# Where the state-space tables are made, when side pieces are emitted, and which queue loads rows and x

## The chip, the cores and the metric

The kernel runs on one core of a Trainium2 chip. The metric is the device time of one execution in microseconds. Its engines are called by the names of the profile: PE (TensorE, the matmuls), DVE (VectorE), ACT (ScalarE), POOL (GpSimd) and SP (SyncE, which here only issues DMAs). DMAs are issued from the queues of SP, ACT and POOL; an engine works its own instructions, DMA issues among them, strictly in order.

## The reference

One layer of a hybrid trunk on a sequence of 512 with 2048 channels, in float32: an adaLN modulation, one wide projection, an S5 state-space mixer and a gated DeltaNet side by side, a gated merge, an output projection, and a SwiGLU feed-forward part.

```python
h  = LN0(x) * (1 + scale_m) + shift_m            # scale, shift, gates = c @ w_ada
p  = h @ W_in      # -> u_ssm | q | k | v | z | beta | a | gate_ssm | gate_gdn
ys = S5(u_ssm): 64 groups x 16 channels, 64 complex states each; GLU; -> 2048
yg = gated DeltaNet: 8 heads, dk = dv = 128, causal conv of 4, chunks of 64; -> 2048
m  = sigmoid(gate_ssm) * ys + sigmoid(gate_gdn) * yg
x  = LN1(alpha * x + gate_m * (m @ W_out))
h  = LN0(x) * (1 + scale_f) + shift_f
x  = LN2(alpha * x + gate_f * SwiGLU(h))
```

The part of S5 that depends on the parameters alone is made once; these are "the state-space tables" below:

```python
dt = exp(log_dt);  mag = exp(lr * dt);  ang = li * dt
ab_re, ab_im = mag * cos(ang), mag * sin(ang)
f = ((ab - 1) * conj(lam)) / |lam|^2             # and powers of ab for the scan
```

## The kernel before

**Matmuls.** Every large product is a float32 product made from three rounded ones (`mm3`, L1130): both sides are split into a high and a low part, and hi*hi, hi*lo and lo*hi go into the same PSUM tile. Such a triple of matmuls, of 512 columns each, is the unit in which the main work advances. Weights come through the class `Weights` (L933-1005): tiles of 512 KB (two halves of 128x1024) are loaded on SP into one of three `raw` buffers, ACT casts them to `whi`, DVE subtracts to `wlo`, and `run_ahead` and a poll keep this two tiles ahead of the matmuls.

**Stages.** The start stage loads x and 64 tiles of `w_ada` (512 KB each, named `wad`), sums the adaLN columns on DVE (`acc`) and PE (`px_adr`), normalizes x, makes h (`hf`, split into `at`), and computes the first six tiles of u. Then come the rest of u and eight DeltaNet heads (the loop at L1468-1480, four gemms each: q, k, v, z). The merge gates, the up-projections, GLU and the merge follow, then the mix-out product (L1687-1716), which goes through four quarters of 512 columns and, in each, twice through pairs of token tiles, so that `w_mix` is loaded twice. At the first pair of a quarter it loads the gate row of that quarter (`row_of`, L1594-1597, into the single buffer `grow`) and tiles of x (L1701). Layer norm halves follow with the rows `ln1_g`, `ln1_b` (L1639-1644). The feed-forward part (L1763-1781) uses `row_of` again, once per quarter and block.

**Side lines and the order.** All instructions go through wrappers (L170 for the engines' operations, L211 for matmuls, L216 for transposes), so most lines of the profile read L170 or L211. The wrappers record each instruction in the class `Order` (L57-152), which keeps a planned clock per engine, with planned durations (L174-189, for POOL 0.2 us plus 0.0021 or 0.0030 us per element of the row). Work beside the main matmuls is written as generators, "lines": the S5 tables `s5_setup` (L272-388), `s5_line` (L551, eight batches), three lines of the DeltaNet, the adaLN rows. After each triple of main matmuls `tick` looks at the lines and emits up to two steps of each line whose planned time `line.t` is far enough in the past:

```python
while n and not line.done and line.t + self.MARGIN <= self.clock:
```

`until` and `drain` emit without that. So the order on every engine is fixed when the kernel is built; on the chip the engines keep it and wait for one another by semaphores. The tables are a line added in the start stage (L1362) and drained at its end (L1395). Most of their arithmetic is on POOL, the sine and cosine on ACT (`sn`, `cs` from `sr`), four transposes on PE into `px_s`, and their results go into `PAr`, `Pi`, `Ftab` and others.

**The adaLN rows in the heads.** `ada_line` (L1167) with `pace` sums 16 tiles (`w1`, 256 KB) into `aacc` on DVE, one each 6.0 us by the plan, and keeps `depth` loads ahead from SP. Without pace it loads from POOL.

Of the kernel before, what the change touches and what calls it, by code (L numbers as in the profile page):

```python
# [11 lines left out]
F32 = mybir.dt.float32  # L12
# [36 lines left out]
def bc(ap, shape):  # L49
    return ap.to_broadcast(shape)  # L50
# [6 lines left out]
class Order:  # L57
# [5 lines left out]
    LAT = 0.12  # L63
    MARGIN = 0.4

# [943 lines left out]
def kernel(ctx, tc, x, c, w_ada, b_ada, w_in, lam_re, lam_im, log_dt, b_re, b_im, c_re, c_im,  # L1009
# [4 lines left out]
    pool_of = lambda **kw: tc.tile_pool(reuse_waits="tile", **kw)  # L1014
# [156 lines left out]
    def ada_line(p, col0, pace):  # L1171
# [7 lines left out]
        deep = k.ada_deep and not pace  # L1179
        depth = 3 if pace else 6 if deep else 4  # L1180
        eng = k.sync if pace else pool
# [60 lines left out]
    cmix = k.per5.tile([128, C_WIDTH - 128], F32, name="cmix")  # L1242
    start, set5 = ExitStack(), ExitStack()
    sp = start.enter_context(pool_of(name="start", bufs=1, side="right"))
    s5p = set5.enter_context(pool_of(name="s5set", bufs=1))
    xs = [[None] * 4 for _ in range(4)]
# [114 lines left out]
    ws.run_ahead()  # L1361
    s5s = o.add(s5_setup(k, s5p, lam_re, lam_im, log_dt))  # L1362
    xnT = []
# [20 lines left out]
    for g in range(4):  # L1384
        o.until(lambda: len(hT) >= 4 * g + 4)
        for k0, nk, cols, u0 in ((0, 2, 512, 0), (2, 2, 512, 0), (0, 4, 256, 4)):
# [7 lines left out]
            ws.run_ahead()  # L1394
    o.drain(s5s)  # L1395
    start.close()
    set5.close()

# [30 lines left out]
    k.tc = lambda n: gp.tile([128, 256], F32, name="g_" + n, tag=n, bufs=1 if n == "X" else 2)  # L1429
    k.sm5 = sp5 = sps.enter_context(pool_of(name="sp5", bufs=1))  # L1430
    alias5 = {"g": "X", "y": "S"}
    alias5w = {"G": "W", "H": "V", "R": "W"}
    k.t5 = lambda n: sp5.tile([128, 512], F32, name="s_" + n, tag="s" + alias5.get(n, n), bufs=2 if n == "U" else 1)
    k.t5w = lambda n: sp5.tile([128, 1024], F32, name="s_" + n, tag="s" + alias5w.get(n, n))
    k.u_done = 0
# [13 lines left out]
    for j in range(6):  # L1449
        u_out(upsum[j])  # L1450
    s5l = o.add(s5_line(k, (b_re, b_im, c_re, c_im), dcol))
    psb = [None]
# [29 lines left out]
    def switch():  # L1482

        o.drain(s5l)
        o.drain(gl)
        sps.close()
        gps.close()
        per5s.close()
        bp = ctx.enter_context(pool_of(name="bp", bufs=32))
        q2 = ctx.enter_context(pool_of(name="q2", bufs=2))  # L1490
        P2.extend((bp, q2))

        def operands():
            for dst, src in ((zs, k.dz), (ygs, k.dy)):
                r = load2(src[0])
                for j in range(8):
                    yield r
                    nxt = load2(src[j + 1]) if j < 7 else None
                    hi, lo = bt(), bt()
                    if dst is zs:  # L1500
                        act.copy(nat(hi), by_pos(r))
                        v.tensor_tensor(out=nat(lo), in0=by_pos(r), in1=nat(hi).bitcast(F32), op=S)
                    else:
                        split(hi, lo, r)
                    dst.append((hi, lo))
                    r = nxt
        k.ada_deep = True
        o.add(operands())
        o.add(ada_rest())
# [88 lines left out]
    def row_to(t, src, q):  # L1598
        ld.dma_start(out=t, in_=bc(src[0:1, 512 * q:512 * q + 512], [128, 512]))
        return t  # L1600
# [30 lines left out]
    def ln_half(hf):  # L1631
# [7 lines left out]
        def row(q):  # L1639
            rows.append((t2("gg"), t2("gs")))  # L1640
            for r, src in zip(rows[q], (ln1_g, ln1_b)):
                ld.dma_start(out=r, in_=bc(src[0:1, 512 * q:512 * q + 512], [128, 512]))
        row(0)
# [43 lines left out]
    for hf in range(2):  # L1687
        for q in range(4):
            sl = slice(512 * q, 512 * q + 512)
            pss = [psum_mm(), psum_mm()]  # L1690
            for c0 in range(0, 16, 2):
                hi, lo = ws.next(2, 512)
                for ti in range(2):
                    ts_ = slice(256 * hf + 128 * ti, 256 * hf + 128 * ti + 128)
                    if c0 == 4:
# [4 lines left out]
                        xa[t][q] = at(F32)  # L1700
                        ld.dma_start(out=xa[t][q], in_=x[0, 128 * t:128 * t + 128, sl])  # L1701
                    for i in range(2):
# [153 lines left out]
```

## Time and profile before

| | us |
|---|---|
| median of 3 runs (lowest to highest) | 3168.74 (3167.68 to 3170.12) |
| the profiled execution | 3170.34 |
| its span in the profile | 3168.6 |
| PE busy in it | 3033.4 (96%) |
| DVE, ACT, POOL busy | 1663.2, 954.5, 782.8 |
| mean granted clock of PE | 0.977 |

A row of the windows has the stretch and its length, then for each engine the busy time and in brackets the number of instructions, then the granted clock (PEclk, 1.00 is full), the mean busy share of the 16 DMA engines and the GB/s that they moved. PEld are PE's weight loads. A row of groups has line, engine, operation, output and inputs with shapes and count, then total and mean (ns) duration, then the idle time of the engine just before these instructions and what ended it. A row of waits reads "who waited <- for whom: total us, how often, longest". In the timeline the first two numbers are the start and the duration. Of a DMA issue the profile has the time of the issuing instruction on the queue's engine (ns: least, median, most) and the time to landing.

### The profile page before, as it was taken

Reading aid. Unit: us, or ns where it says so; the run is one execution under the profiler, and the core shown is the slowest. Engines: PE = TensorE matmul, PEld = TensorE weight load, DVE = VectorE, ACT = ScalarE, POOL = GpSimd, SP = SyncE. Lnnn points to the kernel's source line nnn. Section 1 sums busy time; section 2 is a strip of 40 time slices with the busy share of each in tenths; the row PEclk is TensorE's granted clock in tenths of the full one; section 3 lists DMA queues with packets and bytes.
Section 4 is the critical chain, followed back from the end, with each engine's and each line's share of the span. In section 5 each row is a group of like instructions: output and inputs, shape, how many; then the busy total and the mean of one; then the engine's idle time right before and its main releaser. Section 6 shows DMA issues by size and latency. Waiting matters only on the chain.

```text
span 3168.6 us, 40305 instructions
## 1 busy us (share of the span) xinstructions
PE 3033.4 (96%) x15953; PEld 2499.7 (79%) x15953; DVE 1663.2 (52%) x2217; ACT 954.5 (30%) x1378; POOL 782.8 (25%) x832
## 2 busy tenths in 40 slices
PE   5899989989999999999989999999999999999997
PEld 2588878778777878888769998888888888888885
DVE  6647777666554576756687543333333333333337
ACT  3233333333222343323345631222222222222121
POOL 4834655455112255100022102002001100200202
PEclk8899989999999999999999999999999999999998
DMA  9654334333332688656866553333333333333333
GB/s 330 229 148 110 98 87 111 105 105 95 117 109 84 201 288 288 224 188 207 261 225 192 169 170 103 100 97 110 94 99 110 97 100 101 105 95 102 109 101 120
DMA packets 513534, 458.14 MB, mean 145 GB/s; under 512 B 56145, under 2 KB 403633, under 8 KB 513345
## 3 DMA queue, kind: packets, MB, share of 16 engines
q1 hardware_dynamic: 495904, 408.91, 42.4%
q0 software_dynamic: 10240, 33.56, 3.1%
q10 hardware_dynamic: 7200, 13.10, 1.2%
q8 instruction: 125, 2.05, 0.3%
q14 instruction: 65, 0.52, 0.1%
HBM read 435.60 MB, written 19.89 MB: 144 GB/s over the span
## 4 chain that ended last, share of the span: by engine, by line
PE 64%; DMA 4%; DVE 4%; issue 2%; ACT 2%; POOL 1%; SPq 0%; ACTq 0%; DVEq 0%; POOLq 0%
PE pm L211 47%; PE px_fo L211 14%; DMA raw<-in_w_mix_out_dram 2%; PE px_gd L211 2%; DVE wlo L170 1%; ACT whi L170 1%; DVE at L170 1%; DMA w<-in_w_ada_dram 1%; DVE aacc L170 1%; PE px_ada L211 0%; DMA raw<-in_ffn_w_in_dram 0%; PE px_s L211 0%; ACT f L170 0%; DVE bt L170 0%; DMA g_G<-dG 0%
## 5 line engine op out<-in xcount | busy, mean ns | idle before, releaser
L211 PE MATMUL pm<-at,whi 128*128 128x512 f32 (+1 forms) x3744 | 1145.5, 389 | 8.0 <-ACT whi L170 5.0
L170 DVE TENSOR_TENSOR wlo<-raw,whi 128x1024 fp32r<-128x1024 f32 x541 | 683.4, 1265 | 800.6 <-ACT whi L170 789.7
L170 ACT CAST whi<-raw 128x1024 fp32r<-128x1024 f32 x541 | 567.0, 1050 | 1066.4 <-PE pm L211 454.9
L211 PEld LDWEIGHTS pm<-at,whi 128*128 128x128 f32 x3744 | 683.7, 191 | 137.8 <-ACT whi L170 5.4
L211 PE MATMUL pm<-at,wlo 128*128 128x512 f32 (+1 forms) x1872 | 717.3, 383 | 2.6 <-DVE wlo L170 2.5
L211 PE MATMUL pm<-bt,whi 128*128 128x512 f32 (+1 forms) x2464 | 680.3, 362 | 0.0
L211 PEld LDWEIGHTS pm<-bt,whi 128*128 128x128 f32 x2464 | 442.2, 189 | 71.7 <-issue 0.5
L211 PE MATMUL pm<-bt,wlo 128*128 128x512 f32 (+1 forms) x1232 | 446.0, 362 | 1.5 <-DVE wlo L170 1.5
L211 PEld LDWEIGHTS pm<-at,wlo 128*128 128x128 f32 x1872 | 356.5, 190 | 72.9 <-DVE wlo L170 3.5
L170 POOL TENSOR_TENSOR at<-at,ld 128x512 f32<-128x512 f32 x80 | 120.5, 1538 | 1109.8 <-DVE ld L170 1109.8
L211 PE MATMUL px_fo<-whi,bt 128*128 128x512 f32 x960 | 298.8, 389 | 0.0
L211 PEld LDWEIGHTS pm<-bt,wlo 128*128 128x128 f32 x1232 | 232.9, 189 | 37.8 <-DVE wlo L170 2.2
L211 PEld LDWEIGHTS px_fo<-whi,bt 128*128 128x128 f32 x960 | 180.2, 188 | 37.5
L211 PE MATMUL px_fo<-wlo,bt 128*128 128x512 f32 x480 | 186.7, 389 | 0.0
L170 DVE SCALAR_TENSOR_TENSOR aacc<-w,ccol,aacc 128x512 f32<-128x512 f32 x176 | 163.8, 931 | 6.1 <-DMA w<-in_w_ada_dram 5.1
L170 POOL TENSOR_TENSOR rs<-rs,mhalf 128x1 f32<-128x1 f32 (+1 forms) x13 | 11.3, 872 | 453.1 <-DVE rs L170 453.1
L211 PE MATMUL pm<-whi,bt 128*128 128x512 f32 x336 | 112.5, 405 | 9.8 <-DVE at L170 9.8
L211 PE MATMUL px_fo<-whi,at 128*128 128x512 f32 x336 | 108.2, 392 | 2.0 <-ACT whi L170 2.0
L211 PEld LDWEIGHTS px_fo<-wlo,bt 128*128 128x128 f32 x480 | 90.1, 188 | 18.7
L170 DVE SCALAR_TENSOR_TENSOR gs<-gg,pm 128x512 f32<-128x512 f32 x36 | 24.7, 687 | 142.2 <-ACT gg L170 142.2
L170 DVE TENSOR_TENSOR gs<-gs,pm 128x512 f32<-128x512 f32 x36 | 24.7, 687 | 119.9 <-PE pm L211 119.9
L211 PEld LDWEIGHTS pm<-whi,bt 128*128 128x128 f32 x336 | 64.9, 193 | 26.4 <-DVE at L170 11.7
(412 smaller groups left out, 3232.4 us busy)
## 6 DMA issues: line engine op xcount, KB each, us to landing
raw<-in_ffn_w_in_dram SPq DMA_DIRECT2D x208, 512.0 KB, 4.1
raw<-in_w_in_dram SPq DMA_DIRECT2D x146, 512.0 KB, 4.3
raw<-in_ffn_w_out_dram SPq DMA_DIRECT2D x88, 512.0 KB, 3.7
wad<-in_w_ada_dram SPq DMA_DIRECT2D x64, 512.0 KB, 6.3
w<-in_w_ada_dram SPq DMA_DIRECT2D x128, 256.0 KB, 4.2
raw<-in_w_mix_out_dram SPq DMA_DIRECT2D x64, 512.0 KB, 5.3
w<-in_w_ada_dram POOLq DMA_DIRECT2D x91, 256.0 KB, 4.8
gg<-in_w_ada_dram POOLq DMA_DIRECT2D x37, 256.0 KB, 5.2
```

Source lines behind the costliest of these rows:

```text
L170: r = f(*a, **kw)
L211: r = self.e.matmul(out, **kw)
```

## The change

Four things, and the main matmuls, 12336 of them, stay the same ones:

1. `MARGIN` is 1.0 in place of 0.4 up to `switch` (behind the eight heads), where it is set back to 0.4.
2. The paced adaLN line keeps two loads ahead in place of three.
3. `s5_setup` is no line of the start stage any more. It is the first part of the S5 line, which is added behind the first six u tiles; its memory is released before that of the batches is taken, and both use the same place.
4. The gate rows, `row_to`, the x tiles of the mix-out stage and the rows of the first layer norm are loaded from POOL's queue in place of SP's. Up to the end of the mix-out stage these are 40 DMAs (8 gate rows, 16 x tiles, 16 rows), and `row_to` takes another 32 with it in what follows.

```diff
@@ -61,7 +61,7 @@
 
 
     LAT = 0.12
-    MARGIN = 0.4
+    MARGIN = 1.0
 
     def __init__(self):
         self.free = {"v": 0.0, "a": 0.0, "p": 0.0, "s": 0.0, "pe": 0.0, "d": 0.0}
@@ -1177,7 +1177,7 @@
         acc2 = None if pace else P2[1].tile([128, 512], F32, name="aacc2", tag="aacc2", bufs=1)
         raws = []
         deep = k.ada_deep and not pace
-        depth = 3 if pace else 6 if deep else 4
+        depth = 2 if pace else 6 if deep else 4
         eng = k.sync if pace else pool
 
         def load():
@@ -1240,9 +1240,8 @@
     per5s = ExitStack()
     k.per5 = per5s.enter_context(pool_of(name="per5", bufs=1))
     cmix = k.per5.tile([128, C_WIDTH - 128], F32, name="cmix")
-    start, set5 = ExitStack(), ExitStack()
+    start = ExitStack()
     sp = start.enter_context(pool_of(name="start", bufs=1, side="right"))
-    s5p = set5.enter_context(pool_of(name="s5set", bufs=1))
     xs = [[None] * 4 for _ in range(4)]
     k.sync.dma_start(out=cst, in_=consts[:, 0:128])
     crow = sp.tile([16, 128], F32, name="crow")
@@ -1359,7 +1358,6 @@
     v.tensor_scalar(out=bgl, in0=ps[:, 8:16], scalar1=0.5, scalar2=None, op0=M)
     o.until(lambda: nl.done)
     ws.run_ahead()
-    s5s = o.add(s5_setup(k, s5p, lam_re, lam_im, log_dt))
     xnT = []
     for kt in range(16):
         pt = k.psum("tr")
@@ -1392,9 +1390,7 @@
                     mm3(upsum[u0 + n], wh[:, i, sl], wl[:, i, sl], hT[kt][0], hT[kt][1], kt == 0, kt == 15)
                     o.tick()
             ws.run_ahead()
-    o.drain(s5s)
     start.close()
-    set5.close()
 
 
     adp = ctx.enter_context(pool_of(name="adp", bufs=1, side="right"))
@@ -1427,11 +1423,10 @@
     one_buf = ("E", "wT")
     k.tg = lambda n: gp.tile([128, 512], F32, name="g_" + n, tag=n, bufs=1 if n in one_buf else 2)
     k.tc = lambda n: gp.tile([128, 256], F32, name="g_" + n, tag=n, bufs=1 if n == "X" else 2)
-    k.sm5 = sp5 = sps.enter_context(pool_of(name="sp5", bufs=1))
     alias5 = {"g": "X", "y": "S"}
     alias5w = {"G": "W", "H": "V", "R": "W"}
-    k.t5 = lambda n: sp5.tile([128, 512], F32, name="s_" + n, tag="s" + alias5.get(n, n), bufs=2 if n == "U" else 1)
-    k.t5w = lambda n: sp5.tile([128, 1024], F32, name="s_" + n, tag="s" + alias5w.get(n, n))
+    k.t5 = lambda n: k.sm5.tile([128, 512], F32, name="s_" + n, tag="s" + alias5.get(n, n), bufs=2 if n == "U" else 1)
+    k.t5w = lambda n: k.sm5.tile([128, 1024], F32, name="s_" + n, tag="s" + alias5w.get(n, n))
     k.u_done = 0
     k.fetched = {}
     k.heads, k.heads_ready, k.heads_inverted, k.heads_done, k.gdn_ready, k.cw_ready = {}, 0, 0, 0, False, False
@@ -1448,7 +1443,14 @@
         k.u_done += 1
     for j in range(6):
         u_out(upsum[j])
-    s5l = o.add(s5_line(k, (b_re, b_im, c_re, c_im), dcol))
+
+    def s5_all():
+
+        with pool_of(name="s5set", bufs=1) as s5p:
+            yield from s5_setup(k, s5p, lam_re, lam_im, log_dt)
+        k.sm5 = sps.enter_context(pool_of(name="sp5", bufs=1))
+        yield from s5_line(k, (b_re, b_im, c_re, c_im), dcol)
+    s5l = o.add(s5_all())
     psb = [None]
     o.add(gdn_setup(k, gp, psb, a_log, dt_bias, conv_w, norm_w))
     gemm2(16, hT, lambda n, ps: u_out(ps))
@@ -1483,6 +1485,7 @@
 
         o.drain(s5l)
         o.drain(gl)
+        o.MARGIN = 0.4
         sps.close()
         gps.close()
         per5s.close()
@@ -1596,7 +1599,7 @@
         return row_to(P2[1].tile([128, 512], F32, name="grow", tag="grow", bufs=1), src, q)
 
     def row_to(t, src, q):
-        ld.dma_start(out=t, in_=bc(src[0:1, 512 * q:512 * q + 512], [128, 512]))
+        pool.dma_start(out=t, in_=bc(src[0:1, 512 * q:512 * q + 512], [128, 512]))
         return t
 
 
@@ -1639,7 +1642,7 @@
         def row(q):
             rows.append((t2("gg"), t2("gs")))
             for r, src in zip(rows[q], (ln1_g, ln1_b)):
-                ld.dma_start(out=r, in_=bc(src[0:1, 512 * q:512 * q + 512], [128, 512]))
+                pool.dma_start(out=r, in_=bc(src[0:1, 512 * q:512 * q + 512], [128, 512]))
         row(0)
         row(1)
         st1 = []
@@ -1698,7 +1701,7 @@
                             o.until(lambda: k.ada_m)
                             gm = row_of(drow[2], q)
                         xa[t][q] = at(F32)
-                        ld.dma_start(out=xa[t][q], in_=x[0, 128 * t:128 * t + 128, sl])
+                        pool.dma_start(out=xa[t][q], in_=x[0, 128 * t:128 * t + 128, sl])
                     for i in range(2):
                         a = mT[c0 + i]
                         pe.matmul(pss[ti], lhsT=a[0][:, ts_], rhs=hi[:, i, :], start=(c0 + i == 0), stop=False)
```

The instructions move as follows. First ACT in the start stage before. `whi<-raw` are casts of weights, `hf` and `at` the making of h, `sn` and `cs` sine and cosine for the tables, `part` a sum of the adaLN columns:

```order
L170 CAST whi<-raw 128x1024 x2
L170 ACTIVATE hf<-at,mod_m 128x512
L170 CAST at<-hf 128x512
L170 ACT_TABLE_LOAD
L170 ACTIVATE sn<-sr 64x128
L170 ACTIVATE hf<-at,mod_m 128x512
L170 CAST at<-hf 128x512
L170 ACTIVATE hf<-at,mod_m 128x512
L170 CAST at<-hf 128x512
L170 COPY part<-px_adr 2x512
L170 ACTIVATE cs<-sr 64x128
```

After the change, the same two table rows on ACT stand in the first head, between the activations of its q, k and v (`g_q`, `g_k`, `g_v`):

```order
L170 CAST whi<-raw 128x1024
L170 ACTIVATE g_q<-pm,cw 128x512
L170 CAST whi<-raw 128x1024 x2
L170 ACT_TABLE_LOAD
L170 ACTIVATE sn<-sr 64x128
L170 ACTIVATE g_k<-pm,cw 128x512
L170 CAST whi<-raw 128x1024
L170 ACTIVATE cs<-sr 64x128
L170 CAST whi<-raw 128x1024
```

What stood among the makings of h stands now among the casts of the first head's weights.

Second, PE in the third head before. `g_T`, `g_MT`, `vn` are operands of the DeltaNet's side lines; two rows with `pm` are one triple of main matmuls:

```order
L211 MATMUL px_gd<-St,g_wT 128x128
L211 MATMUL px_go<-St,g_G 128x128
L211 MATMUL px_gd<-g_T,g_MT 64x64 x8
L211 MATMUL pm<-at,whi 128x512 x2
L211 MATMUL pm<-at,wlo 128x512
L211 MATMUL pm<-at,whi 128x512 x2
L211 MATMUL pm<-at,wlo 128x512
L211 MATMUL pm<-at,whi 128x512 x2
L211 MATMUL pm<-at,wlo 128x512
L211 MATMUL px_go<-vn,g_ET 128x128
```

And the same place after the change:

```order
L211 MATMUL px_gd<-St,g_wT 128x128
L211 MATMUL px_go<-St,g_G 128x128
L211 MATMUL px_gd<-g_T,g_MT 64x64 x8
L211 MATMUL pm<-at,whi 128x512 x2
L211 MATMUL pm<-at,wlo 128x512
L211 MATMUL pm<-at,whi 128x512 x2
L211 MATMUL pm<-at,wlo 128x512
L211 MATMUL pm<-at,whi 128x512 x2
L211 MATMUL pm<-at,wlo 128x512
L211 MATMUL pm<-at,whi 128x512 x2
L211 MATMUL pm<-at,wlo 128x512
L211 MATMUL px_gd<-vn,g_kt 128x128
```

Between the product of `g_T` and the next ones that read `vn` there were three triples and are four now.

Third, POOL in the mix-out stage before (`rs` is the layer norm's power, `gg` and `gs` its two affine steps, `aacc` the last adaLN sums). The names behind `aacc` and `w` are buffers:

```order
L170 TENSOR_TENSOR aacc_10595<-aacc_10595,w_10699 128x512
L170 DMA w_10761<-in_w_ada_dram 128x512
L170 DMA w_10778<-in_w_ada_dram 128x512
L170 TENSOR_TENSOR aacc_10595<-aacc_10595,w_10747 128x512
L170 TENSOR_TENSOR rs<-rs,mhalf_137 128x1 x2
L170 TENSOR_TENSOR at<-at,gg 128x512
L170 TENSOR_TENSOR at<-at,gs 128x512
L170 TENSOR_TENSOR at<-at,gg 128x512
L170 TENSOR_TENSOR at<-at,gs 128x512
```

And after the change, in the same stage:

```order
L170 DMA grow<-dgm 128x512
L170 DMA at<-in_x_dram 128x512
L170 TENSOR_TENSOR rs<-rs,mhalf_137 128x1
L170 DMA at<-in_x_dram 128x512
L170 TENSOR_TENSOR rs<-rs,mhalf_137 128x1
L170 DMA gg<-in_ln_g_dram 128x512
L170 DMA gs<-in_ln_b_dram 128x512
L170 TENSOR_TENSOR at<-at,gg 128x512
L170 TENSOR_TENSOR at<-at,gs 128x512
L170 DMA grow<-dgm 128x512
L170 DMA at<-in_x_dram 128x512 x2
L170 DMA gg<-in_ln_g_dram 128x512
```

Gate rows (`grow<-dgm`), x tiles and rows of the layer norm now stand among the layer norm's own steps; from SP's queue they are gone.

## The prediction

> **What bounds the kernel now.** I read the profile page first: PE is busy for nearly all of the span, so what can be won is what PE idles, and what its clock loses. Where that lies shows in the table of windows cut at the stage borders.
>
> ```profile
> span 3168.6 us, 40305 instructions
> PE 3033.4 (96%) x15953; PEld 2499.7 (79%) x15953; DVE 1663.2 (52%) x2217; ACT 954.5 (30%) x1378; POOL 782.8 (25%) x832
> ```
>
> ```profile
> core 0: us, PE busy (x) PEld busy (x) DVE busy (x) ACT busy (x) POOL busy (x), PEclk, DMA share, GB/s
> 0.00:50.00 50.00, 18.00 (x51) 6.82 (x52) 29.66 (x41) 12.68 (x20) 16.24 (x21) 0.91 0.97 332
> 50.00:100.00 50.00, 47.02 (x188) 26.01 (x187) 29.04 (x31) 15.89 (x24) 37.28 (x70) 0.89 0.92 314
> 100.00:150.00 50.00, 39.12 (x131) 23.51 (x130) 30.00 (x29) 16.49 (x27) 43.38 (x68) 0.80 0.66 222
> 150.00:184.00 34.00, 32.18 (x142) 26.21 (x141) 21.06 (x52) 11.21 (x15) 3.12 (x6) 0.90 0.33 102
> 184.00:1060.00 876.00, 837.97 (x5695) 692.99 (x5694) 546.65 (x903) 281.85 (x552) 374.21 (x384) 0.97 0.38 106
> 1060.00:1490.00 430.00, 427.22 (x1903) 353.00 (x1902) 281.38 (x321) 152.38 (x188) 114.10 (x154) 1.00 0.73 242
> 1490.00:1670.00 180.00, 158.55 (x658) 124.53 (x657) 132.40 (x173) 69.52 (x81) 21.13 (x15) 0.95 0.74 240
> 1790.00:3100.00 1310.00, 1310.00 (x6128) 1099.68 (x6126) 454.62 (x471) 309.20 (x343) 120.54 (x80) 1.00 0.36 108
> ```
>
> Up to 100 us the DMA engines are full (0.97 and 0.92 busy, 332 and 314 GB/s): the start stage waits for transfers. From 100 to 150 us they are not (0.66, 222 GB/s), and PE loses 10.9 us besides. In the eight heads (184 to 1060) PE idles 876.00 - 837.97 = 38.0 us and its granted clock is 0.97. In the mix-out stage (1490 to 1670) it idles 21.5 us. The long feed-forward stretch (1790 to 3100) has PE busy for 1310.00 of 1310.00 us at full clock: whatever the change does there can hardly save anything.
>
> Next I looked for what held the start stage while its DMAs were slack: ScalarE's groups of instructions, PE's timeline, SyncE's waits between 50 and 150 us, and from the timeline SyncE's last loads and ScalarE's first output.
>
> ```profile
> L170 ACT ACTIVATE sn<-sr 64x128 f32<-64x128 f32 x1 | 0.3, 311 | 10.0 <-POOL sr L170 10.0
> L170 ACT ACTIVATE cs<-sr 64x128 f32<-64x128 f32 x1 | 0.3, 310 | 4.1 <-POOL sr L170 4.1
> ```
>
> ```profile
> 111.36 1.22 PE L211 MATMUL pm<-at,whi 128*128 128x512 f32 x2 [5.01 <-ACT whi L170]
> 115.13 0.79 PE L211 MATMUL pm<-at,wlo 128*128 128x512 f32 x1 [2.55 <-DVE wlo L170]
> 121.60 0.27 PE L216 MATMUL px_s<-cst,fr 64*128 64x64 f32 x1 [0.42 <-POOL fr L170]
> 124.45 0.27 PE L216 MATMUL px_s<-cst,fi 64*128 64x64 f32 x1 [2.58 <-POOL fi L170]
> ```
>
> ```profile
> SPq L170 <- DVE acc L170: 47.5, 13, 10.2
> ```
>
> ```profile
> 141.12 3.62 SPq L170 DMA_DIRECT2D wad<-in_w_ada_dram  x6
> ```
>
> ```profile
> 183.46 0.36 ACTq L170 DMA_DIRECT2D dup<-g_kb  x1
> ```
>
> ScalarE stands 10.0 us in front of the sine of the state-space tables, since GpSimd has not finished its argument, and 4.1 us in front of the cosine. Behind the sine in ScalarE's order are the casts of the weights and of the input tiles, and PE then stands 5.01 and 2.55 us for a weight tile. VectorE is late with the adaLN sums too, so their buffers come free late, and SyncE stands up to 10.2 us in front of a load: that is how the transfers fall to 222 GB/s. The stage's last loads are issued from 141.12 us on, and its first result (dup) leaves at 183.46. Two transposes of the tables (px_s) cost PE another 0.42 and 2.58 us.
>
> Then PE's waits in the heads, and those of PE and SyncE in the mix-out stage.
>
> ```profile
> PE px_s L216 <- POOL s_V L170: 6.7, 4, 3.8
> PE px_gd L216 <- DVE g_v L170: 5.9, 2, 5.2
> PE px_ada L211 <- DVE aacc L170: 4.6, 1, 4.6
> PE px_gd L211 <- ACT g_th L170: 4.0, 1, 4.0
> PE px_gd L211 <- DVE St L170: 2.8, 1, 2.8
> PE px_gd L211 <- DVE g_T L170: 2.8, 2, 1.7
> PE px_gd L211 <- POOL g_T L170: 2.3, 2, 2.1
> PE px_gd L216 <- ACT g_th L170: 2.3, 1, 2.3
> PE px_gd L216 <- DVE g_k L170: 2.1, 1, 2.1
> ```
>
> ```profile
> PE pm L211 <- DVE at L170: 9.8, 5, 4.1
> PE pm L211 <- DVE wlo L170: 5.5, 7, 1.0
> PE px_ada L211 <- DVE aacc L170: 4.8, 1, 4.8
> PE pm L211 <- ACT whi L170: 1.3, 1, 1.3
> ```
>
> ```profile
> SPq L170 <- DVE wlo L170: 83.6, 47, 6.1
> SPq L170 <- DVE pm L170: 3.5, 4, 2.3
> ```
>
> In the heads no one resource is short. PE arrives at a small side matmul before its operand is there: many waits, each 1 to 5 us, on three engines.
>
> **The change part by part.** The sum is made against the profiled execution's own 3170.34 us, of which 3168.6 is span; the median of the three runs, 3168.74, lies 1.6 us under it, which I take off at the end.
>
> *A. Tables out of the start stage.* What goes from there is all of s5_setup: the POOL work that makes up most of 37.28 and 43.38 us between 50 and 150, the sine, the cosine, some small PSUM copies and transposes, and its loads. The waits that go are 10.0 + 4.1 + 0.42 + 2.58 = 17.1 us, in the order of engines that everything else shares. What comes late next is the transfers. By 150 us the stage has moved 50 x (332 + 314 + 222) = 43.4 MB; the 11.1 MB that were moved between 100 and 150 take 35.4 us at the 314 GB/s of the slice before, 14.6 us less. So the gain is the lower of 17.1 and 14.6: I take -15. It could be -20 if the 2.55 us of wlo goes as well, and only -5 if the casts and adaLN sums that follow turn out to be the pace.
>
> *B. The heads: later pieces, and the tables on top.* MARGIN goes from 0.4 to 1.0: a side piece is emitted once the planner has its operand ready 1.0 us before PE's clock. Ticks come once per triple of matmuls. A matmul takes 427.22 / 1903 = 0.224 us, a triple 0.67 us, so 0.6 us more means about one triple more in front of each piece, as in PE's rows shown with the change, four in place of three. The nine groups of waits quoted above are 16 waits with 33.5 of the 38.0 us. One triple off each is 10.7 us; where a piece lies behind two steps of its line, two triples, 21.4 us; the other 4.5 us, which are short waits, go whole: 15 to 26 us. I take -18, near the lower end, since only the s_V chain over GpSimd has many steps.
>
> The clock adds to that: 0.03 x 876 = 26 us of the stage are lost to a clock of 0.97. If that goes with idle time, 18 / 38 of it, 12 us, come back, if not, nothing; I take the middle, -6. The Trainium skill (TensorE: Matmul & The Clock Gate, Part 1: The HAM clock gate) says that PE falls to half clock after an idle window of about 3.4 us and needs one as long to come back; only the four longest waits above reach that, so by it an estimate would be 4 x 1.7 = 7 us.
>
> Against this stands the tables' work, which now lies among the heads. POOL is busy 374.21 of 876 us there and ACT 281.85, so there is room. In ScalarE's order the sine now stands with casts of weights of head 0 right behind it. These are two tiles ahead; a tile of 512 KB feeds 24 matmuls, 5.4 us, so 10.8 us cover the 10.0 and the 4.1. The cover is not whole, since the casts need their loads too; nothing in the trace of before shows this place. The cost lies between 0 and the same 17.1 us; near a full cover, I take +6. In sum B is -18, with ends at -45 (all idle time, a quarter of the clock loss, no stall) and +10 (tables stall, margin wins little).
>
> The adaLN rows go from 3 buffers to 2 in the heads. One row of them is used every 6.0 us by the planner's pace, and the loads take 4.2 us:
>
> ```profile
> w<-in_w_ada_dram SPq DMA_DIRECT2D x128, 256.0 KB, 4.2
> w<-in_w_ada_dram POOLq DMA_DIRECT2D x91, 256.0 KB, 4.8
> ```
>
> With two buffers a load has 12 us less the time of use: nothing; if it slips, the 4.6 us wait for aacc comes again.
>
> *C. Rows and x loads from GpSimd's queue.* In the mix-out stage SyncE's queue holds nothing but weight loads after the change. SyncE itself waited for buffers (83.6 us behind wlo), 3.5 us only behind the pm readers of a gate row; but weight tiles came late to PE by 5.5 + 1.3 = 6.8 us. If the rows that stood between them made this, it goes: -7. The 9.8 us for at and the 4.8 us for aacc have nothing to do with SyncE's queue and stay. At best all 17 us but aacc go; at worst the loads arrive later, below.
>
> What an issue costs GpSimd:
>
> ```profile
> L170 SPq DMA_DIRECT2D w<-in_w_ada_dram x128: 327/430/1145, 184.7 to 1640.1; - x128
> L170 POOL DMA_DIRECT2D w<-in_w_ada_dram x91: 546/546/566, 1056.8 to 1288.1; - x91
> ```
>
> 0.55 us each, for 40 loads up to the end of the mix-out stage 22 us of an engine that is busy 21.13 of 180 us. That is free. A landing takes 0.6 us more, and the x tiles are asked for long ahead. The 32 feed-forward rows: PE is full there, 0. What GpSimd's queue now has behind each load that waits for a buffer are the layer norm's powers and affine steps, which no matmul of the mix-out stage needs.
>
> A rule that speaks against this: the Trainium skill (SBUF — State Buffer, SBUF: two separate sides) has DMAs that GpSimd issues starve for descriptors while VectorE holds the port they share. The trace doesn't bear it out: the 91 loads above took at most 566 ns to issue in a stretch with VectorE busy 281.38 of 430 us, though a delay after the issue would show only in the 4.8 us.
>
> Sum: 3170.3 - 15 - 18 - 7 = 3130.3; less 1.6, 3129.
>
> **The rivals.** *The stall moves with the tables.* GpSimd is as slow in head 0 as before, the planner still counts it too cheap (one 64x128 step it puts at 0.2 + 128 x 0.003 = 0.58 us), and the sine stands in front of the casts again, where the cover is 10.8 us at most. Then B is nothing: 3170.3 - 15 - 7 - 1.6 = 3147. For it speaks that ScalarE's order is fixed and the wait was 10.0 us; against it the cover and the larger margin, which is meant for just such errors.
>
> *The start stage stays as long.* Transfers, casts and adaLN sums pace it without the tables: A is -5, 3139. For it: SyncE waited for acc 13 times, 47.5 us, and only 10.2 us of that is the one long stall.
>
> *The queue move wins nothing,* because SyncE was held by buffers and not by rows, or because VectorE holds GpSimd's loads back (it is busy 132.40 of 180 us there): C is 0, 3136.
>
> *Slower: GpSimd's queue blocks itself.* The gate row has one buffer. Its next load waits for four VectorE readers of the quarter before, and the x tiles of the next quarter stand behind it in GpSimd's queue; if GpSimd comes there well before VectorE is done, or is held by a power of the layer norm that waits for VectorE, the x tiles and the gate row come late, PSUM is not emptied, and PE stands. A quarter is 45 us; half a quarter lost in three of them is 67 us: 3170.3 - 15 - 18 + 67 - 1.6 = 3203. It decides from 11 us per quarter on. Against it: SyncE in the same place waited 2.3 us at the longest.
>
> *Margin buys nothing.* The waits come back elsewhere, the tables stall, and the start stage gains the least: -5 to 0, 3165 to 3169.
>
> **How the numbers follow.** Forecast 0.45; stall moves 0.22; start stays 0.15; queue move wins nothing 0.05; slower 0.08; nothing at all 0.05. What a measurement of this kernel can tell is some 0.2%, 6.3 us, so faster is under 3162.4 and slower over 3175.1. The first four are faster, but for the tail of the second (0.01): faster 0.86, same 0.06, slower 0.08. The low end has B near -45 with C at -12: 3097; I take 3095. The high end has the stall moved and the start little shortened: 3170.3 - 5 - 5 - 1.6 = 3159, taken as 3160. Outside lie the slower case, most of the last and a little below.
>
> **What would show it.** In the profile after: the window from 100 to 150 us over 300 GB/s and the first dup leaving near 168 instead of 183.46 us (A); PE's idle in the heads near 20 us instead of 38, the waits for s_V, g_v and g_th shorter by a triple each, sn's wait on ScalarE no longer followed by a wait of PE for whi (B); in the mix-out stage no waits of PE for wlo and whi, and idle near 15 us (C). It is wrong if the heads take 876 us or more, if the last start load is still issued behind 141 us, or if PE waits for DVE pm in the mix-out stage.

## The result, and the profile after

The changed kernel takes 3115.11 us (median of 4 runs, 3112.85 to 3116.33), before it was 3168.21 (4 runs); the ratio is 0.9831, 95% interval 0.9814 to 0.9848. The medians are 53.1 us apart. The profiled execution, by which the stages are compared below, is 3112.85 us against 3170.34, 57.5 us less. The table of windows of the kernel after, cut at its own stage borders, has the columns of the prediction's.

```profile
core 0: us, PE busy (x) PEld busy (x) DVE busy (x) ACT busy (x) POOL busy (x), PEclk, DMA share, GB/s
0.00:50.00 50.00, 17.71 (x56) 7.48 (x56) 30.11 (x41) 13.73 (x21) 16.40 (x24) 0.92 0.97 341
50.00:100.00 50.00, 49.89 (x203) 31.72 (x203) 33.76 (x36) 20.16 (x30) 0.00 (x0) 0.91 0.96 334
100.00:122.80 22.80, 22.80 (x91) 13.35 (x90) 18.39 (x20) 6.11 (x8) 0.00 (x0) 0.93 0.97 338
122.80:157.70 34.90, 34.90 (x157) 28.21 (x155) 18.22 (x19) 14.04 (x19) 0.00 (x0) 0.95 0.46 153
157.70:1010.50 852.80, 823.85 (x5668) 685.14 (x5667) 537.39 (x924) 281.31 (x545) 446.15 (x516) 0.98 0.38 108
1440.00:1611.00 171.00, 156.59 (x662) 122.99 (x661) 129.99 (x170) 70.56 (x82) 37.12 (x45) 0.98 0.78 253
3042.00:3111.10 69.10, 45.96 (x180) 34.85 (x179) 54.88 (x81) 11.08 (x17) 19.91 (x15) 0.85 0.24 84
```

In the start stage POOL is idle from 50 us on, the DMAs run at 334 to 338 GB/s to the end of the loads, and PE idles only 0.1 us. From the timelines, the last adaLN loads on SP and the first output on ACT:

```profile
114.85 7.13 SPq L170 DMA_DIRECT2D wad<-in_w_ada_dram  x8
```

```profile
157.13 0.36 ACTq L170 DMA_DIRECT2D dup<-g_kb  x1
```

To add up the stages I cut both kernels at the same events: the first dup, the last load of w_in (the heads and merge gates lie between), the first load of w_mix, the first load of the feed-forward. The same windows of the kernel before, and then of the kernel after:

```profile
183.50:1217.30 1033.80, 993.02 (x6389) 821.23 (x6388) 652.73 (x1013) 348.47 (x636) 447.53 (x485) 0.97 0.45 133
1444.30:1669.90 225.60, 204.15 (x857) 161.91 (x856) 160.94 (x210) 84.37 (x97) 21.03 (x15) 0.96 0.72 232
```

```profile
157.10:1167.80 1010.70, 980.36 (x6387) 814.62 (x6386) 637.61 (x1037) 347.92 (x638) 508.38 (x605) 0.99 0.44 132
1395.40:1609.70 214.30, 200.06 (x852) 158.95 (x850) 157.84 (x204) 83.92 (x95) 35.82 (x44) 0.98 0.74 243
```

| stage | before | after | difference |
|---|---|---|---|
| start, to the first dup | 183.5 | 157.1 | -26.4 |
| heads and merge gates | 1033.8 | 1010.7 | -23.1 |
| up to the first w_mix load | 227.0 | 227.6 | +0.6 |
| mix-out | 225.6 | 214.3 | -11.3 |
| from there to the end | 1498.7 | 1501.4 | +2.7 |
| span | 3168.6 | 3111.1 | -57.5 |

In the heads PE's idle time went from 1033.80 - 993.02 = 40.8 to 1010.70 - 980.36 = 30.3 us, and the same matmuls were 12.7 us shorter. The longest of PE's waits in the kernel after, first in the heads (up to 1010 us), then in the mix-out stage:

```profile
PE px_gd L211 <- POOL g_T L170: 6.0, 3, 3.2
PE px_s L216 <- POOL s_V L170: 5.4, 3, 2.3
PE px_gd L211 <- DVE g_X L170: 3.7, 4, 1.4
PE px_gd L216 <- DVE g_kb L170: 3.1, 1, 3.1
PE px_gd L211 <- DVE vn L170: 2.9, 2, 2.1
PE px_gd L216 <- DVE g_v L170: 2.8, 2, 1.5
PE px_s L216 <- POOL fi L170: 2.2, 1, 2.2
```

```profile
PE pm L211 <- DVE at L170: 8.0, 5, 2.5
PE pm L211 <- ACT whi L170: 2.7, 1, 2.7
PE pm L211 <- DVE wlo L170: 2.7, 6, 0.9
```

The waits for g_th (4.0 and 2.3) and St (2.8) are gone. Those for POOL (g_T, s_V, fi) make 13.6 us. In the mix-out stage the wait for aacc is gone, while 5.4 us of waits for wlo and whi remain.

### The profile page after: what moved, and what is told of

Same layout as the page of the kernel before. It is cut to its first block, busy times and chain, and to the rows that moved or that the text cites. A ratio compares the mean times of both kernels' runs of the same rounds, so it can differ in the third digit from the quotient of the medians.

```text
span 3111.1 us, 40284 instructions
## 1 busy us (share of the span) xinstructions
PE 3005.1 (97%) x15953; PEld 2488.9 (80%) x15953; DVE 1650.4 (53%) x2217; ACT 954.8 (31%) x1378; POOL 810.8 (26%) x904
## 4 chain that ended last, share of the span: by engine, by line
PE 66%; DVE 4%; DMA 3%; issue 2%; ACT 1%; POOL 1%; ACTq 0%; DVEq 0%; SPq 0%; POOLq 0%
PE pm L211 48%; PE px_fo L211 14%; DMA raw<-in_w_mix_out_dram 2%; PE px_gd L211 1%; DVE at L170 1%; DVE wlo L170 1%; ACT whi L170 1%; PE px_s L211 1%; DMA raw<-in_ffn_w_in_dram 1%; DVE aacc L170 0%; DVE st L170 0%; PE px_ada L211 0%; DVE pm L170 0%; DVE raw L170 0%; POOL g_T L170 0%
## 5 line engine op out<-in xcount | busy, mean ns | idle before, releaser
L211 PE MATMUL pm<-at,whi 128*128 128x512 f32 (+1 forms) x3744 | 1133.8, 386 | 0.1
L170 DVE SCALAR_TENSOR_TENSOR aacc<-w,ccol,aacc 128x512 f32<-128x512 f32 x180 | 154.4, 858 | 4.5 <-DMA w<-in_w_ada_dram 3.4
L211 PEld LDWEIGHTS pm<-whi,bt 128*128 128x128 f32 x336 | 63.9, 190 | 23.5 <-DVE at L170 10.2
L211 PEld LDWEIGHTS px_fo<-whi,at 128*128 128x128 f32 x336 | 63.5, 189 | 15.2 <-ACT whi L170 2.1
```

The costliest lines, as they stand in the source:

```text
L170: r = f(*a, **kw)
L211: r = self.e.matmul(out, **kw)
```

## The experiments

All ratios are to the kernel before, on the same chip. The theory behind the runs: the parts of the change add up, one to a stage. Stage times are of the profiled executions, cut as in the table above. Kernels with the same order of instructions up to the end of the mix-out stage (the changed kernel, and the one with its feed-forward rows on SP) differ there by some 1 us.

### The tables alone

The diff of the change without its MARGIN, `depth` and `pool.dma_start` lines.

> The kernel before with one part of the change: the tables are made in the heads, MARGIN stays 0.4, three adaLN loads, rows and x on SP. Theory (the parts add up; the start stage's gain is ScalarE's three waits for the tables, 10.0 + 4.1 + 12.5 = 26.6 us): the first dup leaves near 157 us instead of 183.5, the heads are 0 to 8 us longer, the whole is 18 to 27 us faster, about 3146. Rival (the parts only work together, since with the small margin the tables stall the heads): the heads are 15 us or more longer and the whole is at most 10 us faster, 3158 or more.

Measured: 3147.03 us, ratio 0.9927 (0.9915 to 0.994). The first dup leaves at 155.3 us, 28.2 earlier. The heads take 1032.8 us, as before (1033.8): at the small margin the tables cost them nothing, though the waits are other ones. The mix-out stage is 4.6 us longer (230.2); why was not followed up. The first of PE's waits in the heads:

```profile
PE px_gd L211 <- ACT g_th L170: 17.2, 6, 6.3
PE px_gd L211 <- POOL g_T L170: 10.2, 3, 5.2
PE px_gd L216 <- DVE g_kb L170: 5.2, 1, 5.2
```

The rival falls.

### The margin alone

```diff
-    MARGIN = 0.4
+    MARGIN = 1.0
...
+        o.MARGIN = 0.4      # in switch()
```

> The kernel before with MARGIN 1.0 up to the end of the heads and nothing else. Theory (parts add up): the heads from the last dup to the last w_in load are some 20 us shorter, the start stage 3 to 8 us, as the margin also holds the sine back by a little; the whole 20 to 28 us faster, about 3144. Rival (the gain in the heads came from the tables' departure or the adaLN depth and not from the margin): within 6 us of before.

Measured: 3132.84 us, ratio 0.988 (0.9867 to 0.9893): more than either theory had. Its start stage is 185.7 us, 2.2 longer, so none of it comes from there. The heads and the mix-out stage:

```profile
185.70:1183.60 997.90, 978.20 (x6383) 811.15 (x6382) 638.50 (x1001) 346.01 (x632) 431.71 (x466) 0.99 0.45 133
1411.20:1626.90 215.70, 201.30 (x855) 161.16 (x854) 158.51 (x206) 83.40 (x95) 22.62 (x15) 0.98 0.74 243
```

The heads are 35.9 us shorter: idle 19.7 in place of 40.8 us (-21.1), the matmuls themselves 14.8 us. Of PE's waits there, only these two are for POOL:

```profile
PE px_s L216 <- POOL s_V L170: 1.6, 1, 1.6
PE px_s L211 <- POOL s_X L170: 0.5, 1, 0.5
```

The mix-out stage is 9.9 us shorter, with rows and x still on SP. That is nearly all that the whole change gained there (11.3).

### The queue alone, and everything but the queue

```diff
-        ld.dma_start(out=t, in_=bc(src[0:1, ...
+        pool.dma_start(out=t, in_=bc(src[0:1, ...
```

and likewise the two other loads. The second run undoes the same lines in the changed kernel.

> The kernel before with rows and x loads on GpSimd's queue and nothing else. Theory (the queue gives the mix-out stage's 11 us): 8 to 12 us faster, about 3158, PE's waits for wlo and whi shorter. Rival (the mix-out stage gained because the adaLN rows, by the other parts, came at another place, so that its 4.8 us wait for aacc fell away): 0 to 4 us faster, the aacc wait still there.

> The changed kernel with rows and x loads back on SP's queue. Theory (the queue gives 11 us): 8 to 12 us slower than the changed kernel, about 3125. Rival (the aacc wait gave it): 0 to 4 us slower, 3115 to 3119, with no aacc wait in the mix-out stage.

Measured: the queue alone 3174.8 us, ratio 1.0015 (1.0006 to 1.0024), slower. Its mix-out stage is 222.3 us, 3.3 shorter than before, and still has

```profile
PE px_ada L211 <- DVE aacc L170: 4.8, 1, 4.8
```

but the time from the start of the last px_fo matmul to the end of the span, the close from here on, is 18.2 us, 15.3 before. The changed kernel with rows back on SP takes 3110.66 us, ratio 0.981 (0.9796 to 0.9823), with a mix-out stage of 213.1 us against 214.3 and a close of 14.7 us. So the queue is worth nothing in the mix-out stage of the changed kernel, and costs some 3 us in the close. Both expectations of the theory fall. The rival's hold for the aacc wait, which is there in the first run and not in the second; its times do not, since it gave the queue 0 to 4 us of gain and the queue cost time in both.

### The tables in the start stage, planned dearer

```diff
+            if k == "p":
+                us *= self.o.POOLX       # 1.6 until the tables are drained, then 1.0
```

> The kernel before, tables still made in the start stage, but the planner counts each GpSimd step there 1.6 times as dear, so that the sine, the cosine and the copies of the tables stand later in ScalarE's order, by about the time that GpSimd is late. Theory (the start stage lost 26 us in ScalarE's waits for the tables, 10.0 + 4.1 + 12.5): the waits shrink under 5 us together and the first dup leaves at 158 to 166 us in place of 183.5. Rival (it is the tables' work itself, GpSimd slowing VectorE and a stage that is full): the first dup stays at 175 us or later, though the waits are gone.

Measured: 3142.11 us, ratio 0.9914 (0.9901 to 0.9928); first dup at 177.8 us. Neither theory: the waits did not shrink, they moved.

```profile
L171 ACT ACTIVATE cs<-sr 64x128 f32<-64x128 f32 x1 | 0.3, 312 | 4.1 <-POOL sr L171 4.1
L171 ACT ACTIVATE sn<-sr 64x128 f32<-64x128 f32 x1 | 0.3, 311 | 11.0 <-POOL sr L171 11.0
L171 ACT COPY PAr<-px_s 128x64 f32<-128x64 f32 x1 | 0.3, 272 | 11.2 <-PE px_s L219 11.2
```

The reason is at the head of POOL's chain, which waited for the load of dt 23.1 us here and 9.4 us before:

```profile
POOL er L171 <- DMA dt<-in_ssm_log_dt_dram: 23.1, 1, 23.1
```

So this run did not do what it was meant to. It still shows one thing: with the stalls pushed behind most of the loads, the last wad loads are issued from 112.3 us on, as early as without tables, and yet the first dup is only 5.7 us earlier. The transfers alone don't set the end of the stage. That ScalarE's 26 us of waits set it, wherever they stand, fits this, but no run has the tables in that stage without the waits.

The rest of the gain, 25 us, lies in its heads (1008.5 us in place of 1033.8), at MARGIN 0.4. In PE's order there the pieces of the S5 batches stand later, the first behind 483 main matmuls in place of 426 and the last behind 1773 in place of 1719. Those of the DeltaNet stand earlier at first (the first St piece behind 843 in place of 909) and end at the same place. Which of these shifts gained the 25 us was not isolated.

### POOL's work in the start stage without anyone waiting

POOL gets a line of 120 steps on 64x128 tiles, two to a step of the line, added where the tables' line was. Its core:

```diff
+        for i in range(60):
+            pool.tensor_tensor(out=pw[2], in0=pw[0], in1=pw[1], op=A)
+            pool.tensor_scalar(out=pw[1], in0=pw[0], scalar1=0.5, scalar2=None, op0=M)
+            yield 0.5
```

> The changed kernel with some 80 us of GpSimd arithmetic on small scratch tiles put into the start stage, for which no other engine waits (work added, nothing left out). Theory (waits, not work): VectorE's steps of 128x1024 beside it take 1353 ns in place of 1283 again, which costs 2 to 6 us, first dup at 157 to 163 us. Rival (the work itself): first dup at 175 us or later.

Measured: 3114.07 us, ratio 0.9829 (0.9814 to 0.9844); first dup at 161.7 us, 4.6 later than in the changed kernel. The whole is no slower than the changed kernel (0.9829 against 0.9831): the profiled heads are 4.2 us shorter. POOL is busy for 90.9 us from 50 to 150, where the tables made 80.7. VectorE's groups in the start stage (50 us on) before, after, and in this run:

```profile
L170 DVE SCALAR_TENSOR_TENSOR acc<-wad,ccol,acc 128x1024 f32<-128x1024 f32 x29 | 39.2, 1353 | 3.7 <-DMA wad<-in_w_ada_dram 3.1
L170 DVE TENSOR_TENSOR at<-hf,at 128x512 fp32r<-128x512 f32 x12 | 9.6, 800 | 22.9 <-ACT at L170 22.9
```

```profile
L170 DVE SCALAR_TENSOR_TENSOR acc<-wad,ccol,acc 128x1024 f32<-128x1024 f32 x27 | 34.6, 1283 | 0.6
L170 DVE TENSOR_TENSOR at<-hf,at 128x512 fp32r<-128x512 f32 x11 | 7.6, 689 | 9.3 <-ACT at L170 9.3
```

```profile
L170 DVE SCALAR_TENSOR_TENSOR acc<-wad,ccol,acc 128x1024 f32<-128x1024 f32 x26 | 35.1, 1349 | 0.6
L170 DVE TENSOR_TENSOR at<-hf,at 128x512 fp32r<-128x512 f32 x10 | 8.4, 835 | 10.1 <-ACT at L170 10.1
```

The work itself costs the stage 4.6 us. VectorE's longer steps account for it: 26 x 66 ns, 10 x 146 ns, and 7 subtractions to wlo at 1379 in place of 1219 ns make 4.3 us. So of the 26.4 us some 22 are, by difference, the waits.

### Three adaLN loads, and a margin of 2.0

> The changed kernel with three adaLN loads ahead again. Theory (depth costs nothing; the tables' work costs the heads the 12 us by which the changed kernel's heads lose more than those with the margin alone): within 4 us of the changed kernel, 3111 to 3119. Rival (two buffers make the 12 us): 8 to 13 us faster than the changed kernel, about 3104.

> The changed kernel with MARGIN 2.0 in place of 1.0 up to the end of the heads. Theory (a piece that comes later finds its operand ready; the heads of the changed kernel still idle 30 us): idle in the heads falls to about 18 us, the clock to 0.99, 10 to 16 us faster than the changed kernel, about 3102. Rival (1.0 was enough; what still waits are chains over GpSimd that are late by more, and the lines are now pushed past the end of the heads, where they are drained at a standstill): no gain or slower, 3112 or more, with more idle time behind the heads.

Each is one number in the changed kernel (`depth = 3 if pace`, `MARGIN = 2.0`). Three loads: 3121.38 us, ratio 0.9847 (0.9833 to 0.986), 2 us above the theory's range, with intervals of the two ratios that overlap. The heads are 1011.2 us against 1010.7: depth is not what the heads lose, and the rival falls. The profiled run is longer only behind the first feed-forward load, where PE's first waits for the layer norm's output are 7.4 in place of 2.7 us. These waits vary from kernel to kernel, and that stretch without the close lies between 1481 and 1492 us in the fourteen kernels.

MARGIN 2.0: 3152.09 us, ratio 0.9945 (0.9933 to 0.9958), 37 us worse than the changed kernel. The heads are 7 us shorter (1003.3), the start 6 us longer, and the stretch behind them 264.4 us in place of 227.6, since the side lines end 276 to 318 main matmuls later and the adaLN sums with them:

```profile
PE px_ada L211 <- DVE aacc L170: 16.8, 2, 16.3
PE pm L211 <- ACT whi L170: 7.1, 1, 7.1
```

The rival holds: what a piece's delay buys in the heads is more than given back behind them.

### Feed-forward rows back on SP

```diff
-        pool.dma_start(out=t, ...
+        (pool if src is drow[2] else ld).dma_start(out=t, ...
```

> The changed kernel with the feed-forward's gate rows and the second layer norm's rows back on SP's queue; gate rows, x and layer-norm rows of the mix-out stage stay on GpSimd's. Theory (the queue move cost its 3.0 us at the program's very end and nothing in the mix-out stage): the time from the last px_fo matmul to the end falls from 18.2 to about 15 us, the whole to that of the changed kernel with all rows on SP, 3108 to 3114. Rival (GpSimd's loads in the mix-out stage are what is paid for): the end stays at 18 us.

Measured: 3111.47 us, ratio 0.982 (0.9807 to 0.9834); a close of 15.6 us. The last output leaves SP's queue 3.9 us before the end of the span, before 3.6, in the changed kernel 6.5. The theory holds: the late rows on POOL's queue cost about 3 us in the close.

The traces also show where. Every program ends with a DRAIN instruction on POOL's queue, and the last semaphores of all engines follow it. Before, in the changed kernel, and in this run it lasts (ns: least, median, most of three):

```profile
L1852 POOLq DRAIN  x3: 40/93/3516, 3161.3 to 3168.3; - x3
L1855 POOLq DRAIN  x3: 40/93/9394, 3100.9 to 3110.8; - x3
L1855 POOLq DRAIN  x3: 40/102/6781, 3100.0 to 3107.3; - x3
```

It lasts 3.5 us in the eight kernels with 128 DMAs from POOL's queue, 6.8 us in this one with 168, and 9.4 us in the five with 200: 82 ns more for each further DMA, in both steps. Before, it is over 3.7 us ahead of the end; with 168 or 200 it is over 0.8 us ahead, and SP has waited for it. The added DMAs are all late ones, so their number and their place are not told apart.

### GpSimd planned dearer in the heads, and two more margins

All rows are on SP in these three. One has `POOLX = 1.3` up to `switch`, one `MARGIN = 0.7`, and one leaves MARGIN at 1.0 to the end.

> The changed kernel with all rows on SP, and GpSimd's steps planned 1.3 times as dear up to the end of the heads. Theory (the 12 us that the tables cost the heads at the larger margin are GpSimd, which is planned too cheap and now has the tables among the heads): PE's waits for GpSimd in the heads (g_T, s_V, fi, some 11 to 14 us) fall under 5 us, the heads are 6 to 12 us shorter, 3099 to 3105. Rival (these waits are replaced by others as the order shifts): within 4 us of 3111.

> The changed kernel with all rows on SP and MARGIN 0.7 up to the end of the heads. Theory (each piece of margin takes off a share of each wait): the heads lose some 50 us, between the 62 of 0.4 and the 37 of 1.0, the whole 3118 to 3126. Rival (any shift of the order does it, as the dearer GpSimd plan in the start stage took 25 us from the heads at a margin of 0.4): the heads lose 42 us or less, 3105 to 3115.

> The changed kernel with all rows on SP and MARGIN kept at 1.0 to the end. Theory (the mix-out stage idles like the heads, on side pieces that come too early: 12.8 us there, 7.5 of them on at): 3 to 8 us faster, about 3105. Rival (the mix-out waits are for main operands, at and weights, which no margin moves): within 3 us of 3111.

POOL planned 1.3 times as dear: 3096.64 us, ratio 0.9774 (0.9761 to 0.9788), the fastest of all: by the two ratios 0.0036 x 3170 = 11.4 us under the changed kernel with rows on SP. Its heads, and the first of PE's waits there:

```profile
160.20:1143.00 982.80, 969.36 (x6378) 806.65 (x6377) 621.67 (x1022) 342.97 (x630) 490.63 (x588) 1.00 0.45 131
```

```profile
PE px_ada L214 <- DVE aacc L171: 4.3, 2, 2.8
PE px_gd L214 <- DVE g_X L171: 2.3, 2, 1.3
PE px_gd L214 <- DVE vn L171: 1.6, 2, 1.0
```

The waits for g_T, s_V and fi are down to 0.6 us (0.8 for another of POOL's tiles, g_TT), idle time is 13.4 us at a clock of 1.00, and the heads are 25 us shorter than with rows on SP alone (1007.8). The theory holds, and had half the size. The whole gains less than the heads: the start stage and the mix-out stage are 2.5 us longer each, and the last stretch 3.4.

MARGIN 0.7: 3125.93 us, ratio 0.9865 (0.9852 to 0.9879); heads of 1020.5 us, between 1032.8 with the tables at 0.4 and 1007.8 at 1.0, as the theory had it; the rival falls. Their idle time is 37.9 us, though, hardly less than at 0.4 (40.0): here the gain is almost all in the length of the matmuls (982.6 in place of 992.8 us). MARGIN 1.0 to the end: 3113.28 us, ratio 0.9826 (0.9813 to 0.984): no gain, as the rival had it, though its mix-out stage is 3 us shorter.

## Why the prediction was right, and where its steps failed

**The direction and the total.** -57.5 us in the profiled runs, -53.1 by the medians, where the sum had -40. A and B had the right mechanism and were too small; C was too small and had the wrong cause; the end, put at nothing, costs. That the total lies in the range owes most to A and B. That C came near its figure is luck. By the ratios, the tables alone give -23.1, the margin alone -38.0 and the queue alone +4.8, together -56.4, and the whole -53.6: the parts nearly add up in the total, but not one to a stage, as the margin gives in two of them and the tables cost the heads nothing alone and 12.8 us on top of the margin.

**A, -15, measured -26.4.** The mechanism was right: transfers at full rate to the end, no stall. The step that failed is the size, twice. The waits that go were counted as 17.1 us, with the table transposes at PE's 0.42 and 2.58; but ScalarE stood 12.5 us for those same transposes:

```profile
L170 ACT COPY PAr<-px_s 128x64 f32<-128x64 f32 x1 | 0.3, 278 | 12.5 <-PE px_s L216 12.5
```

10.0 + 4.1 + 12.5 is 26.6. And the bound of 14.6 us took 314 GB/s as the full rate, from a slice in which POOL was already at work. At the rates of the kernel after (341, 334 and 338 GB/s) the same 43.4 MB would be done after some 129 us, by estimate, 21 us before the 150. The run with the dearer plan in the start stage speaks against taking the lower of the two at all: its loads were early and the stage hardly shorter. Of the 26.4 us, 4.6 are POOL's arithmetic beside VectorE (the run with idle work), which the sum didn't have.

**B, -18, measured -23.1.** The sum came out within 5 us, of three terms of which the first alone was close: idle time -18, measured -21.1 with the margin alone; clock -6, measured -14.8; the tables' cost +6, measured +12.8 (1010.7 against 997.9 us). The errors of the other two, -8.8 and +6.8, cancel, which is luck. The clock term was the middle of a range of 0 to 12, and the run with the margin alone lies above its top. The prediction's own sign, idle near 20 us in the heads, did not come in the changed kernel: from 157.7 to 1010.5 us it is 852.80 - 823.85 = 29.0.

As for the margin, "one triple more in front of each piece" holds for one step. Along a line the delay adds up: with the margin alone the last piece of the S5 line stands behind 2043 main matmuls in place of 1848, the DeltaNet's behind 2790 in place of 2712. This is what the run with a margin of 2.0 ran out of.

As for the clock, the trace records when it was granted by half. In the heads before, that was ten times for 3.4 to 10.2 us each, 54.6 us in all, which loses 27.3. With the margin alone it was four times, 20.5 us; in the changed kernel six times, 27.3 us; with POOL planned dearer once, 3.4 us. Not one of PE's waits in the heads with the margin alone is longer than 3.1 us. One of its four falls, 2.6 us of wait (for St) in the stretch ahead of it, then the half clock, then the full one:

```profile
462.80:466.20 3.40, 1.27 (x9) 1.13 (x10) 3.37 (x6) 0.00 (x0) 0.73 (x1) 0.99 0.00 0
466.20:469.60 3.40, 3.40 (x10) 2.63 (x9) 3.23 (x10) 1.61 (x9) 0.45 (x1) 0.50 0.49 140
469.60:473.00 3.40, 3.40 (x23) 3.02 (x22) 2.77 (x8) 1.38 (x4) 0.59 (x1) 1.00 0.58 148
```

The Trainium skill (TensorE: Matmul & The Clock Gate, Part 1: The HAM clock gate) has the half clock follow an idle window of about 3.4 us, by which I estimated 7 us from the four longest waits. The trace disagrees in size: waits of 2 to 3 us also bring a fall here, and a fall lasts 5.5 us on average, not 3.4. Idle time and clock don't go strictly together: at a margin of 0.7 the heads idle 37.9 us and their matmuls take 982.6 us, in the changed kernel 30.3 and 980.4.

The tables' cover of two split tiles (128x1024, 512 KB each) held, in the part that was feared. ScalarE waits for the sine again in head 0, 8.4 and 5.7 us, and PE does not wait for whi: its waits there are 3.1 us for g_kb and 2.2 for fi, one of the tables. ScalarE's rows in the kernel after, from 157 to 260 us:

```profile
L170 ACT ACTIVATE sn<-sr 64x128 f32<-64x128 f32 x1 | 0.3, 311 | 8.4 <-POOL sr L170 8.4
L170 ACT ACTIVATE cs<-sr 64x128 f32<-64x128 f32 x1 | 0.3, 311 | 5.7 <-POOL sr L170 5.7
L170 ACT COPY PAr<-px_s 128x64 f32<-128x64 f32 x1 | 0.3, 285 | 3.2 <-PE px_s L216 3.2
```

The 12.8 us are paid later, and to POOL: PE's waits for it in the heads are 2.1 us with the margin alone and 13.6 in the changed kernel, 11.5 more, where all idle time is 10.6 more. Behind the tables the eight batches lie within 1392 main matmuls in place of 1476 with the margin alone, and POOL is planned too cheap (`g_E<-g_G,gcol` 128x128 took 815 ns where the plan has 0.58 us). Planning it dearer removes these waits and more, 25 us; how much of the 25 is the tables' wasn't separated.

**C, -7 by the queue, measured -11.3, which stays with the rows on SP.** This step was wrong. The prediction tied PE's 6.8 us for wlo and whi to the rows among SP's loads, although SP itself waited for buffers, and 5.4 us of these waits are still there. It also said the aacc wait would stay, and that is the one that went. It is there in the three runs at MARGIN 0.4 with the order of before (before, tables, queue alone) and at most 1.0 us in those at a larger margin: in PE's order the last adaLN row stands behind 5328 main matmuls or more there, and behind 5151 before. That accounts for 4.8 of the 11.3 us. The rest (wlo, clock) comes with the margin too, which alone gives 9.9 of the 11.3, and what of the order makes it wasn't isolated; the run with the dearer plan in the start stage lost the aacc wait with the row still at 5151, so the place alone doesn't settle it.

**The end, 0, measured +2.7.** Wrong too: the close is 2.9 us longer (18.2 in place of 15.3), by POOL's DRAIN. The stretch ahead of it is the same, 1483.2 and 1483.4 us. The prediction asked only whether a load would be late for its matmul.

**Rivals.** That the queue wins nothing was given 0.05 and is what happened, inside a sum that the other terms carried. The stall did move with the tables, 8.4 and 5.7 us of it at ScalarE, but without PE waiting behind it. The blocked queue did not come: PE never waited for DVE's pm in the mix-out stage. (The stage goes through the four quarters twice, with eight gate rows, so a turn is 28 us and not the 45 of that rival.)

## What to carry to other kernels

When work leaves an in-order engine, add up that engine's own waits for it, not only the waits that the bottleneck shows. Where many small waits on different engines idle the bottleneck, look at the plan that orders the work before the hardware: here planning one engine's steps 1.3 times as long was worth 11 us on top of the margin. A margin for all pieces is a coarser cure, which turned to loss (at 2.0) when the side lines ran out of main work to hide behind. A change of several parts is judged part by part: one of the four here cost time and was carried by the others.

## What the runs showed of the hardware

VectorE's steps get slower while GpSimd computes: 128x1024 steps 1283 to 1349 ns, 128x512 splits 689 to 835 ns, with GpSimd work that nobody waits for. The Trainium skill (SBUF — State Buffer, SBUF: two separate sides) has the two share a port that one of them holds for a whole instruction; this trace agrees in that VectorE's steps with two inputs get slower; for how long the port is held it doesn't show. The starving of DMAs that GpSimd issues, from the same section, did not show in the mix-out stage (214.3 us with them, 213.1 without). What does show is the close: with 200 DMAs from GpSimd's queue in place of 128, its closing DRAIN lasts 9.4 us in place of 3.5, and the span ends 6.5 us after the last output is issued in place of 3.6. What the DRAIN does in that time is open.

The clock of PE was granted by half for 3.4 to 10.2 us at a time in the heads, also behind waits of 2 to 3 us; with fewer such waits it fell four times in place of ten.
